# A macaron block on one core: 128 tokens left unturned at the end, one table load moved, queries and keys rounded for both heads at once

## The chip, the core and the metric

The kernel runs on one core of a Trainium2 chip. The metric is the device time of one execution in microseconds (us). TensorE does the matrix products (PE in the profile, PEld for its weight loads), VectorE (DVE) and ScalarE (ACT) the elementwise work, GpSimd (POOL) a little, and SyncE (SP) issues most of the transfers (DMAs) between HBM and the on-chip memory SBUF, and within SBUF. Products land in PSUM.

## What is computed

One transformer block over 512 tokens of width 1024, in float32: half a SwiGLU feed-forward, an attention mixer, half a second feed-forward, and a last norm.

```python
x = x + 0.5 * swiglu(rmsnorm(x, ffn1_norm), w_gate1, w_up1, w_down1)
x = x + token_mixer(rmsnorm(x, mix_norm), w_in, w_out, lambdas, subln_gain, rel_bias)
x = x + 0.5 * swiglu(rmsnorm(x, ffn2_norm), w_gate2, w_up2, w_down2)
return rmsnorm(x, final_norm)      # out: [1, 512, 1024]
```

The mixer has four differential heads (two softmaxes of 64-wide queries and keys each, the second subtracted with a learned factor) and eight dilated heads of width 64. All are causal, with a bias by distance. In the kernel they are eight pairs of 64-wide heads, `u` = 0 to 7: the first four pairs are the differential heads, the last four are the dilated ones.

## The kernel before

**Number format.** Every float32 value is kept as two parts: a high part rounded to the fast float32r format (`A.copy` into a float32r tile, a CAST in the profile) and a low part, value minus high (a subtraction on VectorE). A product of two values takes three TensorE passes (`mm3`, L152 to L154). Residual `x` lies transposed: eight tiles `x[m]` of 128 features by 512 tokens. Tokens 0 to 255 are the slice `left`, tokens 256 to 511 the slice `right`.

**Order.** TensorE's order is the order in which the code is written, everywhere. In the mixer VectorE's and ScalarE's is too; there the code runs through numbered chunks (`put(t, rank, ...)` hangs a step on chunk `t`, and steps with rank under 10 come ahead of the chunk's products, in order of rank). One unit of eight chunks makes the queries and keys of a pair (`q0` to `q7`), or half of the values (`v0` to `v3`), in the order v0 q0 q1 v1 q2 q3 q4 v2 q5 q6 v3 q7. A chunk is some 1.3 to 1.5 us of TensorE. The queues of SP and GpSimd are ordered by the framework's scheduler; each issues in that order, and a transfer that must wait holds what is behind it.

**Queries and keys of a pair.** `qk_chunks(u)` forms them. With `e` the pair's last chunk, `scaled` (L1055, L1057) writes `tq` and `tk`, 128 partitions by 512 tokens: partitions 0 to 63 (`lo`) belong to head 0 and 64 to 127 (`hi`) to head 1. The scores need six tiles. `q0` holds head 0's high part in `lo` and its low part in `hi`; `q1` the same for head 1 with the halves exchanged. `k0` and `k1` hold one head's high part in both halves, `l0` and `l1` its low part in both halves. So one pass over 128 partitions multiplies both parts of the query with the key's high part (L1227), and a second one with its low part (L1228). The tiles were filled in three ways:

- pairs 1 to 4 (`evac_q`, `evac_k`, `evac_rests`): each head by itself, 64 partitions at a time; four casts on ScalarE, four subtractions on VectorE, all written where they belong, and four SBUF-to-SBUF transfers (L1073) for the second halves of `k` and `l`;
- pairs 5 and 6 (`SPREAD`): keys rounded for both heads at once into `kh` and `kl` and sent by eight transfers (L1109); queries a head at a time in place;
- pairs 0 and 7 (`evac_now`): no transfers.

The first scores of a pair (`score`) stand at chunk `e` + 6, in `attention`. The softmax follows, with exponentials on ScalarE (L1232), weights turned by TensorE (`turn`, into `pt`), copied to `ptb` by ScalarE (L1256), and multiplied with the values (`values`, L1267).

**The last FFN and the end.** The second FFN ends with three plain products p5, p6, p7 (one output tile each) and four units `d` by a seven-product scheme. `squared` adds the squares for the last norm as each `x[m]` becomes final. Its root is a Sqrt on ScalarE, whose table differs from that of Silu, so a one-element Sqrt into `root` brought the table in ahead of time, after the square of tile 1. In `final_end` the 256 `left` tokens were scaled as they lie, features on partitions (`final_left`; the factors spread over partitions by a product with ones, `final_spread`), and stored transposed, so that the host turned them. The 256 `right` tokens were turned by 16 TensorE transposes (`final_turn`), scaled out of PSUM (`final_right`) and stored as rows.

Of the kernel before, what the change touches and what calls it, by code (L numbers as in the profile page):

```python
# [21 lines left out]
P = 128  # L22
# [60 lines left out]
def tile_macaron(ctx: ExitStack, tc, xs, xT, wf, wgu1, wst1, wd1, wdg1, wqk, wv, wo, wgu2, wst2, wd2,  # L83
# [153 lines left out]
    def ffn(wgu, wst, wd, wdg, n0, n1, norm, early, res, nm, hooks, ended, first=None,  # L237
# [426 lines left out]
        def schedule():  # L664
            seen = {}
            for t, (u, o) in enumerate(ops):
# [4 lines left out]
                else:  # L671
# [26 lines left out]
                    else:  # L698
                        at(starts[t] - 3 * STEP, 2.5, low, t)
                at(starts[t], 4, product, t)  # L700
            if bias is not None:
                at(starts[begin["p", 5]], 5, bias[0])
                at(starts[begin["p", 7]], 5, bias[1])
                at(starts[begin["p", 6]] + STEP, 5, bias[3])
                at(starts[begin["d", 1, 0] + 2], 5, bias[2])
# [327 lines left out]
    def qk_chunks(u):  # L1033
# [25 lines left out]

        def evac_q():  # L1060
            q0, q1, k0, k1, l0, l1 = tiles()
            tq, tk = scaled()
            A.copy(k0[lo, :], tk[lo, :])
            A.copy(k1[hi, :], tk[hi, :])
            A.copy(q0[lo, :], tq[lo, :])
            A.copy(q1[hi, :], tq[hi, :])

        def evac_k():
            q0, q1, k0, k1, l0, l1 = qk[u]
            tq, tk = st["tq"], st["tk"]  # L1070

            def other_half(t, a, b):
                nc.sync.dma_start(t[b, :].bitcast(F32), t[a, :].bitcast(F32))  # L1073

            other_half(k0, lo, hi)
            other_half(k1, hi, lo)
            for a, b, kx, lx in ((lo, hi, k0, l0), (hi, lo, k1, l1)):
                V.tensor_tensor(lx[a, :], tk[a, :], kx[a, :].bitcast(F32), op=ALU.subtract)
                other_half(lx, a, b)

        def evac_rests():
            q0, q1, k0, k1, l0, l1 = qk[u]
            tq = st["tq"]
            for a, b, qx in ((lo, hi, q0), (hi, lo, q1)):
                V.tensor_tensor(qx[b, :], tq[a, :], qx[a, :].bitcast(F32), op=ALU.subtract)

        def evac_now():
# [15 lines left out]
        elif u in DIRECT:  # L1103
            put(e, 11, evac_now)
        elif u in SPREAD:
            def send(t, *places):
                for o, a in zip(places, (lo, hi)):
                    for b in (lo, hi):
                        nc.sync.dma_start(o[b, :].bitcast(F32), t[a, :].bitcast(F32))  # L1109

            def cast_k():
                q0, q1, k0, k1, l0, l1 = tiles()
                t = st["kh"] = slot(0, f"kh{u}", F32R)
                A.copy(t[:], st["tk"][:])
                send(t, k0, k1)

            def low_k():
                q0, q1, k0, k1, l0, l1 = qk[u]
                t = slot(1, f"kl{u}", F32R)
                V.tensor_tensor(t[:], st["tk"][:], st["kh"][:].bitcast(F32), op=ALU.subtract)  # L1120
                send(t, l0, l1)

            def cast_q(n):
                a = (lo, hi)[n]
                A.copy(qk[u][n][a, :], st["tq"][a, :])

# [76 lines left out]
    def attention(u, s):  # L1203
# [205 lines left out]
        for i in range(NQ):  # L1409
# [320 lines left out]
    def final_dg():  # L1730
        n = NQ // 2
        dg = fin["dg"] = tp.tile([P, S], F32, tag="ptb", name="dgl")
        V.tensor_tensor(dg[:, :HS].rearrange("p (i q) -> p i q", i=n),
                        ident[:].rearrange("p (o q) -> p o q", o=1).to_broadcast([P, n, P]),
                        fin["y", 0][:].rearrange("p (i o) -> p i o", o=1).to_broadcast([P, n, P]),
                        op=ALU.mult)

    def final_spread():
        fin["pb"] = pp.tile([P, S], F32, tag="mm", name="bcl", bufs=4)[:, :HS]
        for c in (slice(0, P), slice(P, HS)):  # L1740
            T.matmul(fin["pb"][:, c], ones_m, fin["dg"][:, c], start=True, stop=True)


    def final_left(a):
        if a != 3:
            fin["left"] = wp.tile([P, 1024], F32, tag="raw", name=f"yl{a}")
        y = fin["left"][:, a // 3 * S:a // 3 * S + S].rearrange("p (m q) -> p m q", m=2)
        x2 = x_all[:, 2 * a * S:2 * (a + 1) * S].rearrange("p (m q) -> p m q", m=2)[:, :, left]
        f = fin["pb"].rearrange("p (o q) -> p o q", o=1).to_broadcast([P, 2, HS])
        V.tensor_tensor(y, x2, f, op=ALU.mult)  # L1750
        if a != 2:
            n = 1 + a // 3
            nc.sync.dma_start(out[0, 2 * (a + 1) - 2 * n:2 * (a + 1)].rearrange("m p q -> p m q"),
                              fin["left"][:, :n * S].rearrange("p (m q) -> p m q", q=HS))


    def final_turn(i, ms):
        for m in ms:
            h = m // 4
            if (i, h) not in fin:  # L1760
                tag = {(0, 0): "mm", (1, 0): "s", (0, 1): "s", (1, 1): "t"}[i, h]
                fin[i, h] = pp.tile([P, S], F32, tag=tag, name=f"xt{i}{h}", bufs=4 if tag == "mm" else 2)
            T.transpose(fin[i, h][:, m % 4 * P:(m % 4 + 1) * P],
                        x[m][:, HS + i * P:HS + (i + 1) * P], ident[:])
# [10 lines left out]

    def wd_tile(i):
        return tp.tile([P, 1280], F32, tag=f"pr{i}", name=f"yr{i}")

    def final_store(i, c, queue):
        o = out[1].rearrange("k p q -> (k p q)").rearrange("(t d) -> t d", d=D)  # L1780
        queue.dma_start(o[i * P:(i + 1) * P, c], fin["out", i][:, c])

    def final_end():
        q6, q7 = fin["sq"]
        every = slice(0, S)
        weigh(KD - 1, right, V)
        weigh(KD - 2, right)
        final_means(1, sq, end=False)
        final_spread()
        final_turn(0, range(2))  # L1790
        final_means(1, q6, first=False)
        final_left(0)
        final_roots(1)
# [6 lines left out]
        final_left(1)  # L1800
        final_right(0, 1, every, A)
        final_store(0, slice(0, D), nc.sync)
        final_left(2)
        final_left(3)
        final_right(1, 0, every, A)
        final_store(1, every, nc.sync)
        final_right(1, 1, right, V)
        final_right(1, 1, left, A)
        final_store(1, slice(S, D), nc.scalar)

# [112 lines left out]
```

## Time and profile before

| what | value |
|---|---|
| time, median of 3 runs | 890.2 us (889.88 to 890.86) |
| the profiled execution's own time | 890.6 us |
| its span in the profile | 887.7 us |
| HBM read, written | 137.28 MB, 2.14 MB |
| granted TensorE clock, mean | 0.997 of full speed |

Rows of a timeline give the start (us from the span's start), the duration, the engine, the line, the operation with output <- inputs, and in brackets how long the engine stood idle before it and for whom. Rows of waits give who waited <- for whom: us in total, times, longest. Rows of a group give minimum/median/maximum in ns, or in `--lines` form the busy us, mean ns, and idle time before. Rows of `windows` give a stretch, then the busy time of each engine, the granted clock, the share of the transfer engines' time and GB/s.

### The profile page before, as it was taken

To read this page: it belongs to the slowest core of one execution; us is meant where nothing else is said; L and a number is where in the kernel's file an instruction comes from. 1 tells how busy PE (TensorE), PEld (TensorE's weight loads), DVE (VectorE), ACT (ScalarE), POOL (GpSimd) and SP (SyncE) were. 2 spreads that over 40 slices of the span, in tenths; PEclk is the share of its full clock that TensorE was granted. 3 is DMA by queue.
4 is the path that set the end of the run, shared out by engine and by line. 5 is a ranking of instruction groups with operands and counts; after the bars stand their busy time and mean duration, and the time that the engine had idled before them with its cause. 6 is when DMAs were issued, how large, how long until landed. Compare 5 with 4: busy or idle time off the path is not lost.

```text
span 887.7 us, 17743 instructions
## 1 busy us (share of the span) xinstructions
PE 875.6 (99%) x6558; PEld 834.5 (94%) x6558; DVE 755.1 (85%) x1590; ACT 550.7 (62%) x1162; POOL 111.2 (13%) x140
## 2 busy tenths in 40 slices
PE   9999999999999999999999999999999999999996
PEld 8889999999999999998989889889999999999996
DVE  7799998787998995788997859999899678799786
ACT  7456674455765764666766858466667355666474
POOL 0011101012103100001010220011110111211100
PEclk9999999999999999999999999999999999999998
DMA  8456756688857842445365664656783857884842
GB/s 279 125 168 157 177 142 184 148 212 213 201 141 211 222 132 95 119 131 156 106 174 149 183 139 120 176 158 152 185 212 97 201 169 187 216 224 118 215 127 95
DMA packets 65685, 146.85 MB, mean 165 GB/s; under 512 B 7632, under 2 KB 8912, under 8 KB 65600
## 3 DMA queue, kind: packets, MB, share of 16 engines
q1 hardware_dynamic: 47840, 113.02, 39.2%
q0 software_dynamic: 17616, 32.45, 22.7%
q8 instruction: 51, 0.84, 0.4%
q14 instruction: 34, 0.28, 0.1%
q10 hardware_dynamic: 144, 0.26, 0.1%
HBM read 137.28 MB, written 2.14 MB: 157 GB/s over the span
## 4 chain that ended last, share of the span: by engine, by line
PE 82%; DVE 10%; ACT 4%; issue 2%; DMA 1%; SPq 0%; DVEq 0%; ACTq 0%
PE po L1267 2%; PE pdb L154 1%; DVE w L948 1%; PE pdb L153 1%; PE pdb L152 1%; DVE w L445 1%; PE pv L1012 1%; PE pv L1014 1%; PE pv L1013 1%; PE pygb L152 1%; PE pwgb L154 1%; PE pxgb L154 1%; PE pyub L154 1%; PE pyub L153 1%; PE pxub L154 1%
## 5 line engine op out<-in xcount | busy, mean ns | idle before, releaser
L1232 ACT ACTIVATE pr<-pr,small 128x128 f32<-128x128 f32 (+3 forms) x64 | 35.7, 559 | 31.4 <-DVE small L1229 31.1
L441 ACT CAST w<-s2b 128x512 fp32r<-128x512 f32 x52 | 32.4, 623 | 22.0 <-DVE s2b L423 19.9
L441 ACT CAST w<-s2a 128x512 fp32r<-128x512 f32 x48 | 29.8, 623 | 23.3 <-DVE s2a L423 19.7
L445 DVE TENSOR_TENSOR w<-s2b,w 128x512 fp32r<-128x512 f32 x52 | 35.6, 685 | 0.9 <-ACT w L441 0.6
L1012 PE MATMUL pv<-w,xh 128*128 128x256 f32 x128 | 35.7, 279 | 0.0
L1229 DVE CUSTOM_DVE_ANT_0 pr<-sc,strip 128x128 f32<-128x128 f32 (+3 forms) x64 | 29.5, 485 | 7.2 <-PE sc L1228 7.0
L1014 PE MATMUL pv<-w,xh 128*128 128x256 f32 x128 | 35.1, 274 | 0.0
L1013 PE MATMUL pv<-w,xl 128*128 128x256 f32 x128 | 35.1, 274 | 0.0
L445 DVE TENSOR_TENSOR w<-s2a,w 128x512 fp32r<-128x512 f32 x48 | 32.8, 684 | 0.8 <-ACT w L441 0.6
L152 PE MATMUL pq<-xh,w 128*128 128x512 f32 x64 | 25.6, 401 | 0.0
L948 DVE TENSOR_TENSOR w<-raw_qk,w 128x512 fp32r<-128x512 f32 x32 | 21.7, 686 | 4.5 <-ACT w L944 4.5
L1013 PEld LDWEIGHTS pv<-w,xl 128*128 128x128 f32 x128 | 24.5, 191 | 0.1
L1012 PEld LDWEIGHTS pv<-w,xh 128*128 128x128 f32 x128 | 24.5, 191 | 0.1
L1014 PEld LDWEIGHTS pv<-w,xh 128*128 128x128 f32 x128 | 24.5, 191 | 0.0
L152 PE MATMUL pk<-xh,w 128*128 128x512 f32 x64 | 24.3, 380 | 0.0
L154 PE MATMUL pq<-xh,w 128*128 128x512 f32 x64 | 24.3, 379 | 0.0
L153 PE MATMUL pk<-xl,w 128*128 128x512 f32 x64 | 24.3, 379 | 0.0
L154 PE MATMUL pk<-xh,w 128*128 128x512 f32 x64 | 24.3, 379 | 0.0
L153 PE MATMUL pq<-xl,w 128*128 128x512 f32 x64 | 24.3, 379 | 0.0
L1267 PEld LDWEIGHTS po<-v,ptb 128*128 128x128 f32 x160 | 21.5, 191 | 2.6 <-ACT ptb L1256 1.6
L944 ACT CAST w<-raw_qk 128x512 fp32r<-128x512 f32 x32 | 19.3, 615 | 6.2 <-PE pv L1013 2.8
L1267 PE MATMUL po<-v,ptb 128*128 128x128 f32 (+1 forms) x160 | 22.0, 272 | 1.0 <-ACT ptb L1256 1.0
(826 smaller groups left out, 4096.5 us busy)
## 6 DMA issues: line engine op xcount, KB each, us to landing
raw_qk<-wqk_dram SPq DMA_DIRECT2D x16, 512.0 KB, 3.8
raw0bg<-wst_dram SPq DMA_DIRECT2D x9, 512.0 KB, 5.0
raw0bu<-wst_dram SPq DMA_DIRECT2D x9, 512.0 KB, 5.7
raw_gua<-wgu_dram SPq DMA_DIRECT2D x8, 512.0 KB, 3.6
raw0ag<-wst_dram SPq DMA_DIRECT2D x8, 512.0 KB, 5.0
raw0au<-wst_dram SPq DMA_DIRECT2D x8, 512.0 KB, 5.2
raw0ad<-wdg_dram SPq DMA_DIRECT2D x8, 512.0 KB, 5.9
strip<-bias_rows SPq DMA_DIRECT2D x16, 256.0 KB, 4.0
```

The source lines that it names most:

```text
L152: T.matmul(po, wh, mh, start=first, stop=False, skip_group_check=on)
L153: T.matmul(po, wh, ml, start=False, stop=False, skip_group_check=on)
L154: T.matmul(po, wl, mh, start=False, stop=last, skip_group_check=on)
L441: A.copy(made[t][0], source(t))
L445: V.tensor_tensor(l, source(t), h.bitcast(F32), op=ALU.subtract)
L948: V.tensor_tensor(l[:, c:c + 512], raw[:, c:c + 512], h[:, c:c + 512].bitcast(F32), op=ALU.subtract)
L1012: T.matmul(po, xh[k][:, xs], mh_, start=k == 0, stop=False)
L1013: T.matmul(po, xl[k][:, xs], mh_, start=False, stop=False)
L1014: T.matmul(po, xh[k][:, xs], ml_, start=False, stop=k == KD - 1)
L1229: V.tensor_tensor_reduce(out=o, in0=a, in1=b, op0=ALU.add, op1=ALU.min, scale=1.0, scalar=3.0e38, accum_out=st["mx"][:, m, i:i + 1])
L1232: A.activation(pi, pi, AF.Exp, scale=-1.0, bias=st["mx"][:, m, i:i + 1], accum_out=st["ls"][:, m, i:i + 1])
L1267: T.matmul(st["po3"][:, i, d0:d0 + dn], st["ptb", m, i][:, k * P:(k + 1) * P], vk, start=k == 0, stop=k == i)
```

## The change

Four edits:

1. `root`'s one-element Sqrt, and the table load with it, moves from the square of tile 1 to the start of p6, after p6's products in the order of the code.
2. Pairs 1 to 6 all fill their tiles in one way. `cast_k` and `cast_q` round both heads at once, 128 partitions, into `kh` and `qh`; `low_k` and `low_q` subtract both at once into `kl` and `ql`. Everything is then placed by transfers: four for `kh`, four for `kl`, two for `qh`, two for `ql`, twelve for a pair. (Pairs 1 to 4 had four, pairs 5 and 6 eight.)
3. The first value products of pair 0 stand one chunk earlier.
4. At the end only tokens 0 to 127 stay unturned; tokens 128 to 511 are turned by 24 transposes. The output is one [512, 1024] array of rows, in which the first 128 rows hold the unturned block, re-ordered on the host.

```diff
@@ schedule, in ffn
+            if last is not None:
+                at(starts[begin["p", 6]], 5, lambda: A.activation(root[:], eps[:], AF.Sqrt))
@@ squared
             put(t + STEP, A.activation, sq[:], x[m], AF.Square)
-            if not mixer:
-                put(t + STEP, A.activation, root[:], eps[:], AF.Sqrt)
             put(t + 2 * STEP, weighted)
@@ qk_chunks
-        def evac_q():
...
-        def evac_k():
...
-        def evac_rests():
...
-        elif u in SPREAD:
+        else:
+            kt, lt, qt, rt = (20, 21, 22, 23) if u < 5 else (0, 1, 2, 3)
+
             def send(t, *places):
-                for o, a in zip(places, (lo, hi)):
-                    for b in (lo, hi):
-                        nc.sync.dma_start(o[b, :].bitcast(F32), t[a, :].bitcast(F32))
+                for a, o in zip((lo, hi), places):
+                    for p, b in o:
+                        nc.sync.dma_start(p[b, :].bitcast(F32), t[a, :].bitcast(F32))
 
             def cast_k():
                 q0, q1, k0, k1, l0, l1 = tiles()
-                t = st["kh"] = slot(0, f"kh{u}", F32R)
+                t = st["kh"] = slot(kt, f"kh{u}", F32R)
                 A.copy(t[:], st["tk"][:])
-                send(t, k0, k1)
+                send(t, ((k0, lo), (k0, hi)), ((k1, lo), (k1, hi)))
...
-            def cast_q(n):
-                a = (lo, hi)[n]
-                A.copy(qk[u][n][a, :], st["tq"][a, :])
-
-            def low_q(n):
-                a, b = ((lo, hi), (hi, lo))[n]
-                V.tensor_tensor(qk[u][n][b, :], st["tq"][a, :], qk[u][n][a, :].bitcast(F32),
-                                op=ALU.subtract)
+            def cast_q():
+                q0, q1 = qk[u][:2]
+                t = st["qh"] = slot(qt, f"qh{u}", F32R)
+                A.copy(t[:], st["tq"][:])
+                send(t, ((q0, lo),), ((q1, hi),))
+
+            def low_q():
+                q0, q1 = qk[u][:2]
+                t = slot(rt, f"ql{u}", F32R)
+                V.tensor_tensor(t[:], st["tq"][:], st["qh"][:].bitcast(F32), op=ALU.subtract)
+                send(t, ((q0, hi),), ((q1, lo),))
 
             put(e, 11, scaled)
             put(e + 1, 6.7, cast_k)
+            put(e + 2, 6.7, cast_q)
             put(e + 2, 7, low_k)
-            for n in range(2):
-                put(e + 2 + n, 6.7, cast_q, n)
-                put(e + 3 + n, 11, low_q, n)
-        else:
-            put(e, 11, evac_q)
-            put(e + 1, 11, evac_k)
-            put(e + 2, 7, evac_rests)
+            put(e + 3, 7, low_q)
@@ attention
-                put(tv + 2 * i + (3 if (u, i) in ((0, 0), (1, NQ - 1)) else 2), 1, values, 0, i)
+                put(tv + 2 * i + (3 if (u, i) == (1, NQ - 1) else 2), 1, values, 0, i)
@@ the end
+        y = wp.tile([P, 1024], F32, tag="raw", name=f"yl{a}")[:, :S]
+        x4 = x_all[:, 4 * a * S:4 * (a + 1) * S].rearrange("p (m q) -> p m q", m=4)[:, :, :P]
...
+        V.tensor_tensor(y.rearrange("p (m q) -> p m q", m=4), x4, f, op=ALU.mult)
+        nc.sync.dma_start(out[:P, a * S:(a + 1) * S], y)
@@ final_end
         weigh(KD - 1, right, V)
-        weigh(KD - 2, right)
+        final_turn(1, range(4))
+        final_spread()
         final_means(1, sq, end=False)
-        final_spread()
-        final_turn(0, range(2))
         final_means(1, q6, first=False)
         final_left(0)
+        final_rows(1, 0, A)
+        final_store(1, 0, nc.sync)
+        final_left(1)
         final_roots(1)
-        final_turn(0, (2, 3, 4, 5, 7))
...
+        weigh(KD - 2, right)
+        final_turn(1, range(4, 8))
+        final_turn(2, range(4))
+        final_turn(3, range(4))
+        final_turn(2, (4, 5, 7, 6))
+        final_turn(3, (4, 5, 7, 6))
         final_factors(1)
-        final_right(0, 0, every, A)
...
+        final_rows(1, 1, A)
+        final_store(1, 1, nc.sync)
+        final_rows(2, 0, V)
+        final_store(2, 0, nc.sync)
+        final_rows(3, 0, V)
+        final_rows(2, 1, A)
+        final_store(2, 1, nc.sync)
+        final_store(3, 0, nc.sync)
+        final_rows(3, 1, V, right)
+        final_rows(3, 1, A, left)
+        final_store(3, 1, nc.scalar)
```

`_OUT_SHAPE` and the host's last lines follow the new layout.

**SP's queue at pair 1, before.** The rows are the transfers that SP issues between two weight loads of the mixer (`raw_qk`); `k` and `l` are the key tiles, a number names a buffer, and `strip` is a bias strip of a later pair.

```order
L139 DMA raw_qk_4672<-wqk_dram 128x1024
L1073 DMA k_4457<-k_4457 64x512
L1073 DMA k_4458<-k_4458 64x512
L1073 DMA l_4459<-l_4459 64x512
L1073 DMA l_4460<-l_4460 64x512
L878 DMA strip_4882<-bias_rows 128x512
L878 DMA strip_4884<-bias_rows 128x512
L139 DMA raw_qk_4680<-wqk_dram 128x1024
```

**The same place after the change.** `q_4469` and `q_4470` are the query tiles of the two heads.

```order
L139 DMA raw_qk_4680<-wqk_dram 128x1024
L1083 DMA k_4471<-kh_4475 64x512 x2
L1083 DMA k_4472<-kh_4475 64x512 x2
L1083 DMA q_4469<-qh_4504 64x512
L1083 DMA q_4470<-qh_4504 64x512
L1083 DMA l_4473<-kl_4508 64x512 x2
L1083 DMA l_4474<-kl_4508 64x512 x2
L1083 DMA q_4469<-ql_4546 64x512
L1083 DMA q_4470<-ql_4546 64x512
L139 DMA raw_qk_4688<-wqk_dram 128x1024
L880 DMA strip_4894<-bias_rows 128x512
L880 DMA strip_4896<-bias_rows 128x512
```

Four transfers became twelve, and the low halves of the queries are the last two. Two strips and a load of weights stand behind them.

**ScalarE at pair 1, before.** These are its casts of keys and queries, among the exponentials of pair 0 (`pr`) and the copy of turned weights (`ptb`).

```order
L1232 ACTIVATE pr_4379,small_4380<-pr_4379,small_4380 128x256
L1063 CAST k_4457<-tk_4462 64x512
L1064 CAST k_4458<-tk_4462 64x512
L1065 CAST q_4455<-tq_4461 64x512
L1066 CAST q_4456<-tq_4461 64x512
L1232 ACTIVATE pr_4378,small_4380<-pr_4378,small_4380 128x384
L1232 ACTIVATE pr_4379,small_4380<-pr_4379,small_4380 128x384
L944 CAST w<-raw_qk_4412 128x512
L1256 COPY ptb_4503<-pt_4501 128x128
```

**The same place after the change.**

```order
L1204 ACTIVATE pr_4379,small_4380<-pr_4379,small_4380 128x256
L1204 ACTIVATE pr_4378,small_4380<-pr_4378,small_4380 128x384
L1204 ACTIVATE pr_4379,small_4380<-pr_4379,small_4380 128x384
L1088 CAST kh_4475<-tk_4456 128x512
L944 CAST w<-raw_qk_4412 128x512
L1228 COPY ptb_4499<-pt_4497 128x128
L1100 CAST qh_4504<-tq_4455 128x512
```

Two casts of 128 partitions took the place of four of 64; the first stands behind two exponentials that it stood ahead of, and the second behind the copy. In the same stretch TensorE's order differs only in the value product of pair 0 that stands a chunk earlier; its scores of pair 1 stand where they stood.

More of the change, by code (lines that the diff above doesn't have):

```diff
@@ L1058, in scaled @@
             return tq, tk
-        def evac_q():
[L1061 to L1066, printed above, removed]
-        def evac_k():
[L1069 to L1079, printed above, removed]
-        def evac_rests():
[L1082 to L1085, printed above, removed]
         def evac_now():
@@ L1111, in cast_k @@
             def cast_k():
                 q0, q1, k0, k1, l0, l1 = tiles()
-                t = st["kh"] = slot(0, f"kh{u}", F32R)
+                t = st["kh"] = slot(kt, f"kh{u}", F32R)
                 A.copy(t[:], st["tk"][:])
-                send(t, k0, k1)
+                send(t, ((k0, lo), (k0, hi)), ((k1, lo), (k1, hi)))
             def low_k():
                 q0, q1, k0, k1, l0, l1 = qk[u]
-                t = slot(1, f"kl{u}", F32R)
+                t = slot(lt, f"kl{u}", F32R)
@@ L1120, in low_k @@
                 V.tensor_tensor(t[:], st["tk"][:], st["kh"][:].bitcast(F32), op=ALU.subtract)
-                send(t, l0, l1)
-            def cast_q(n):
-                a = (lo, hi)[n]
-                A.copy(qk[u][n][a, :], st["tq"][a, :])
-            def low_q(n):
-                a, b = ((lo, hi), (hi, lo))[n]
-                V.tensor_tensor(qk[u][n][b, :], st["tq"][a, :], qk[u][n][a, :].bitcast(F32),
-                                op=ALU.subtract)
+                send(t, ((l0, lo), (l0, hi)), ((l1, lo), (l1, hi)))
@@ L1730, in final_dg @@
     def final_dg():
-        n = NQ // 2
         dg = fin["dg"] = tp.tile([P, S], F32, tag="ptb", name="dgl")
[L1733 to L1736, printed above, removed]
+        V.tensor_scalar_mul(dg[:, :P], ident[:], fin["y", 0][:, 0:1])
     def final_spread():
-        fin["pb"] = pp.tile([P, S], F32, tag="mm", name="bcl", bufs=4)[:, :HS]
-        for c in (slice(0, P), slice(P, HS)):
-            T.matmul(fin["pb"][:, c], ones_m, fin["dg"][:, c], start=True, stop=True)
+        fin["pb"] = pp.tile([P, S], F32, tag="mm", name="bcl", bufs=4)[:, :P]
+        T.matmul(fin["pb"], ones_m, fin["dg"][:, :P], start=True, stop=True)
     def final_left(a):
[L1745 to L1754, printed above, removed]
+        y = wp.tile([P, 1024], F32, tag="raw", name=f"yl{a}")[:, :S]
+        x4 = x_all[:, 4 * a * S:4 * (a + 1) * S].rearrange("p (m q) -> p m q", m=4)[:, :, :P]
+        f = fin["pb"].rearrange("p (o q) -> p o q", o=1).to_broadcast([P, 4, P])
+        V.tensor_tensor(y.rearrange("p (m q) -> p m q", m=4), x4, f, op=ALU.mult)
+        nc.sync.dma_start(out[:P, a * S:(a + 1) * S], y)
     def final_turn(i, ms):
@@ L1760, in final_turn, with final_rows @@
             if (i, h) not in fin:
-                tag = {(0, 0): "mm", (1, 0): "s", (0, 1): "s", (1, 1): "t"}[i, h]
+                tag = {(1, 0): "mm", (1, 1): "s", (2, 0): "s", (2, 1): "t", (3, 0): "t", (3, 1): "mm"}[i, h]
                 fin[i, h] = pp.tile([P, S], F32, tag=tag, name=f"xt{i}{h}", bufs=4 if tag == "mm" else 2)
             T.transpose(fin[i, h][:, m % 4 * P:(m % 4 + 1) * P],
-                        x[m][:, HS + i * P:HS + (i + 1) * P], ident[:])
-    def final_right(i, h, c, engine):
-        ps, f = fin[i, h], fin["y", 1][:, i:i + 1]
+                        x[m][:, i * P:(i + 1) * P], ident[:])
+    def final_rows(i, h, engine, c=slice(0, S)):
+        ps, f = fin[i, h], fin["y", i // 2][:, i % 2:i % 2 + 1]
         if ("out", i) not in fin:
-            fin["out", i] = wd_tile(i)
+            fin["out", i] = tp.tile([P, 1280], F32, tag=f"pr{i % 2}", name=f"yr{i}")
         y = fin["out", i][:, h * S:(h + 1) * S]
@@ L1774, in final_right, with final_store @@
             V.tensor_scalar_mul(y[:, c], ps[:, c], f)
[L1776 to L1781, printed above, removed]
+    def final_store(i, h, queue):
+        c = slice(h * S, (h + 1) * S)
+        queue.dma_start(out[i * P:(i + 1) * P, c], fin["out", i][:, c])
     def final_end():
         q6, q7 = fin["sq"]
-        every = slice(0, S)
         weigh(KD - 1, right, V)
-        weigh(KD - 2, right)
+        final_turn(1, range(4))
+        final_spread()
         final_means(1, sq, end=False)
-        final_spread()
-        final_turn(0, range(2))
         final_means(1, q6, first=False)
         final_left(0)
+        final_rows(1, 0, A)
+        final_store(1, 0, nc.sync)
+        final_left(1)
         final_roots(1)
-        final_turn(0, (2, 3, 4, 5, 7))
-        final_turn(1, range(4))
-        final_turn(0, (6,))
-        final_turn(1, (4, 5, 7, 6))
-        final_factors(1)
-        final_right(0, 0, every, A)
[L1800 to L1809, printed above, removed]
+        weigh(KD - 2, right)
[4 more added lines that the diff above has]
+        final_turn(3, (4, 5, 7, 6))
+        final_factors(1)
+        final_rows(1, 1, A)
[9 more added lines that the diff above has]
+        final_store(3, 1, nc.scalar)
     n3 = {}
@@ L1818 @@
         "lams", "relb", "onehot", "addc"]
-_OUT_SHAPE = [2, KD, P, S // 2]
+_OUT_SHAPE = [S, D]
 def _bucket(n):
@@ L1921 @@
     y = r.results[0]["out_0_dram"]
-    return np.concatenate([np.roll(y[0], 1, axis=0).reshape(D, S // 2).T, y[1].reshape(S // 2, D)])[None]
+    first = np.roll(y[:P].reshape(P, KD, P), 1, axis=1).transpose(2, 1, 0).reshape(P, D)
+    return np.concatenate([first, y[P:]])[None]
```

1 line of the change is left out of this document (removed).

## The prediction

> **What bounds the kernel.** I read the busy line of the page, then TensorE's waits, then the chain that ended last, and after them the rows around each wait.
>
> ```profile
> PE 875.6 (99%) x6558; PEld 834.5 (94%) x6558; DVE 755.1 (85%) x1590; ACT 550.7 (62%) x1162; POOL 111.2 (13%) x140
> ...
> PE po L1267 <- ACT ptb L1256: 1.0, 2, 0.5
> PE pt L1350 <- DVE tx L1358: 0.5, 1, 0.5
> PE pt L1250 <- DVE tx L1358: 0.3, 1, 0.3
> PE pydb L152 <- ACT pydb L470: 0.3, 1, 0.3
> ...
> 847.30 1.27 ACT L470
> ```
>
> TensorE is busy for 99% of 887.7 us, and its order of work is written out by hand. So work saved on VectorE or ScalarE is worth only what it removes from TensorE's own waits, and those are small: 1.0 + 0.5 + 0.3 us in the mixer and 0.3 us in the last FFN. The last row is the unnamed 1.27 us at the head of a ScalarE chain near the end: the table load before `root`. Anything that makes TensorE wait anew costs its full length, since no idle time later takes it back.
>
> **The terms that gain.** These are the rows where TensorE stands still in the mixer and at the table load.
>
> ```profile
> 370.19 0.71 PE L1267 MATMUL po<-v,ptb 128*128 128x128 f32 x4 [0.47 <-ACT ptb L1256]
> 413.06 0.49 PE L1267 MATMUL po<-v,ptb 128*128 128x128 f32 x2 [0.51 <-ACT ptb L1256]
> 481.63 0.52 PE L1350 MATMUL pt<-ident,pr 128*128 128x128 f32 x3 [0.53 <-DVE tx L1358]
> 852.97 0.38 PE L152 MATMUL pydb<-h3b,w 128*128 128x256 f32 x1 [0.32 <-ACT pydb L470]
> 829.07 0.62 ACT L608 CAST h3b<-g0b 128x512 fp32r<-128x512 f32 x1 [2.32 <-DVE g0b L479]
> ...
> L1063 ACT CAST k<-tk x4: 617/619/621, 362.4 to 422.4; 64x512 fp32r<-64x512 f32 x4
> L1114 ACT CAST kh<-tk x2: 601/610/620, 457.8 to 472.2; 128x512 fp32r<-128x512 f32 x2
> L1078 DVE TENSOR_TENSOR l<-tk,k x8: 680/688/691, 363.2 to 423.8; 64x512 fp32r<-64x512 f32 x8
> ```
>
> A cast over 64 partitions costs 0.62 us and one over 128 costs 0.61; the subtraction is 0.69 either way. Pairs 1 to 4 go from four casts and four subtractions to two and two, pairs 5 and 6 save one of each: 10 x 0.62 = 6.2 us of ScalarE and 10 x 0.69 = 6.9 us of VectorE. Nearly all of it lies beside TensorE. What counts is that the copy of `ptb` which holds up 370.19 and 413.06, and the `tx` which holds up 481.63, each move up by 0.6 to 1.3 us, so these three waits go. Only the third is a clean gain, **-0.5 us**; the first two sit just ahead of new waits and are counted there. The (0,0) values go one chunk earlier; their `ptb` copy moves up with the casts that no longer stand before it, so I cost that at nothing. The table load leaves 847.30 and stands beside a row that had 2.32 us of idle time before it: **-0.4 us** (0.32 and the refill behind it), and 1.3 us of late casts there if that idle time is gone.
>
> **The term that costs: twelve transfers on one queue.** All of them go through SP.
>
> ```profile
> L1109 SPq DMA_DIRECT2D k<-kh x8: 467/573/602, 458.4 to 474.6; - x8
> L1109 SPq DMA_DIRECT2D l<-kl x8: 467/562/589, 461.2 to 477.2; - x8
> ...
> DMA to landing us min/median/max: 2.3/2.4/4.7
> ...
> L139 SPq DMA_DIRECT2D raw_qk<-wqk_dram x16: 327/330/1126, 322.3 to 463.9; - x16
> ...
> 458.42 2.40 SPq L1109 DMA_DIRECT2D k<-kh  x4
> 472.82 2.40 SPq L1109 DMA_DIRECT2D k<-kh  x4
> ```
>
> These sends exist already for pairs 5 and 6. Four in a row take 2.40 us, so SP issues one each 0.60 us, and each lands 2.4 us after its issue. Before, a pair had four or eight; now every one of pairs 1 to 6 has twelve: 40 more, 24 us of SP time. The score of head 0 reads the whole query tile, high half and low half, so it cannot start before the eleventh send has landed: 10 x 0.60 + 2.4 = 8.4 us after `kh` is cast, and head 1's 9.0 us. In the old form queries never left the engines, and the keys needed only four sends. TensorE's order is the same, so its scores stand where they stood. These rows give the end of `tk` and the first score of each pair (for 1 to 3 that of head 1 too).
>
> ```profile
> 361.64 0.68 DVE L1057 TENSOR_TENSOR tk<-pk,rbc_n 128x512 f32<-128x512 f32 x1
> 371.31 0.28 PE L1227 MATMUL sc<-k,q 128*128 128x256 f32 x1
> 392.28 0.68 DVE L1057 TENSOR_TENSOR tk<-pk,rbc_n 128x512 f32<-128x512 f32 x1
> 400.12 0.28 PE L1227 MATMUL sc<-k,q 128*128 128x256 f32 x1
> 400.36 0.28 PE L1227 MATMUL sc<-k,q 128*128 128x256 f32 x1
> 406.67 0.68 DVE L1057 TENSOR_TENSOR tk<-pk,rbc_n 128x512 f32<-128x512 f32 x1
> 416.02 0.39 PE L1227 MATMUL sc<-k,q 128*128 128x256 f32 x1
> 421.67 0.69 DVE L1057 TENSOR_TENSOR tk<-pk,rbc_n 128x512 f32<-128x512 f32 x1
> 432.23 0.28 PE L1227 MATMUL sc<-k,q 128*128 128x256 f32 x1
> 464.70 0.28 PE L1227 MATMUL sc<-k,q 128*128 128x256 f32 x1
> 481.90 0.37 PE L1227 MATMUL sc<-k,q 128*128 128x256 f32 x1
> ...
> L1232 ACT ACTIVATE pr<-pr,small 128x384 f32<-128x384 f32 x12 | 7.3, 611 | 5.2 <-DVE small L1229 5.1
> L1307 ACT ACTIVATE mh<-ot,few 128x512 fp32r<-128x512 f32 x4 | 2.8, 691 | 0.0
> L1256 ACT COPY ptb<-pt x11: 252/369/586, 366.6 to 418.9; 128x128 f32<-128x128 f32 x3, 128x256 f32<-128x256 f32 x3, 128x384 f32<-128x384 f32 x3, 128x512 f32<-128x512 f32 x2
> ```
>
> - Pair 1: `tk` ends at 362.3; `kh` now stands behind two exponentials of 0.61, which start half a microsecond later, so it ends near 364.7. Head 1's last send lands at 364.7 + 9.0 = 373.7, against a score at 371.31: **+2.4**.
> - Pair 2: `tk` ends at 393.0, and `kh` is behind the copy of `ptb` (0.59) and `mh` (0.69), which wait for TensorE until about 392.5: 394.4. Head 1 lands at 403.4, against 400.36: **+3.0**.
> - Pair 3: `tk` ends at 407.35 and `kh` at 408.0, so 417.0 against 416.02, +1.0. But VectorE's backlog ahead of this `tk` shrinks by about the microsecond, and then it is nothing. I take **+0.5**.
> - Pair 4: `kh` ends at about 424.0 behind a copy of `ptb`; the cast of the queries is behind two exponentials, at 426.9, and SP stands for it. Six sends follow before head 0's last: 426.9 + 6 x 0.60 + 2.4 = 432.9 against 432.23, **+0.7**. Head 1's score is chunks later.
> - Pair 5: the first send stands at 458.42, so 466.8 against 464.70: **+2.1**.
> - Pair 6: 472.82 + 8.4 = 481.2 against 481.90: **0**.
>
> Together +8.7 us (2.4 + 3.0 + 0.5 + 0.7 + 2.1). While a score waits, everything behind it on TensorE waits; VectorE and ScalarE run ahead and then starve. The weight loads and bias strips that queue behind the sends on SP come up to 7 us later, but they are read a whole pair later, so I cost them at nothing.
>
> For bounds: at the fastest issue (0.47) and the 2.3 landing the waits shrink to +0.9, +1.5, -0.5, 0 and +0.7, +2.6 in all (10 x 0.47 + 2.3 = 7.0 after `kh` for head 0, 7.5 for head 1); at the slowest landing (4.7) five heads would add 11.5. The medians stand for sends in a row, which these are, so I take 0.60 and 2.4.
>
> **The tail.**
>
> ```profile
> 878.60 1.73 PE L1763 MATMUL xt<-ident,x 128*128 128x128 f32 x14
> ...
> 878.88 2.03 SPq L1753 DMA_DIRECT2D out_dram<-yl  x2
> ...
> 882.61 0.38 ACTq L1781 DMA_DIRECT2D out_dram<-yr  x1
> ...
> 882.00:884.00 2.00, 0.00 (x0) 0.00 (x0) 0.07 (x1) 0.47 (x1) 0.00 (x0) 0.80 1.02 388
> 886.00:888.00 2.00, 0.00 (x0) 0.00 (x0) 0.00 (x0) 0.00 (x0) 0.00 (x0) 0.50 0.07 26
> ...
> 883.00:883.50 0.50, 0.00 (x0) 0.00 (x0) 0.00 (x0) 0.00 (x0) 0.00 (x0) 0.70 0.91 367
> ```
>
> The end is bound by the 2.1 MB of output: at 388 GB/s 256 KB take 0.67 us, and most of it is issued after 881. Now four blocks (two `yl`, and rows 1 with the factors that are known already) go out from 878.9 on, where the first store stands now, and the last issue falls from 882.61 to about 882.0. The transposes after the sum go from 14 to 20, 0.7 us more, beside the factors. Eight blocks of 0.67 from 879.6 end near 885.0; before, data flowed until about 886.2 (the row from 886 on has 26 GB/s for two microseconds, 52 KB): **-1.2 us**, between 0 and -2.
>
> **Sum:** +8.7 - 0.5 - 0.4 - 1.2 = **+6.6 us**. On the profiled execution's own 890.6 (span 887.7 and 2.9 around it) that is 897.2; that execution is 0.4 above the median of the runs, 890.2, so the forecast is **896.8 us**.
>
> **Rivals.**
> 1. *The sends are in time* (ends faster). If SP issued them as fast as its weight loads, 0.33 us, head 0 would have its queries 3.3 + 2.4 = 5.7 us after `kh`: 370.4, 400.1 and 464.1 for pairs 1, 2 and 5, no later than the scores. All gains would stay: 0.6 at 370, 1.2 at 413 and the two scores behind it (416.02 stands 0.6 later than its chunk needs), then 0.5 + 0.4 + 1.2 as above: 3.9, so 886.3 us. It decides at an issue of about 0.35. The rows of the sends, 0.56 to 0.60, speak against it. 8%. [...]
> 2. *Every send is as short as the shortest seen* (0.47, 2.3): +2.6 - 2.1 = +0.5, 890.7 us. 15%.
> 3. *The clock falls in the new waits.* The granted clock went to half at 883.2 (mean 0.70 in the last row), 2.9 us after the last transpose at 880.3. The waits of pairs 1 and 2 are 2.6 to 2.7 us long, just short of it. If they count, TensorE runs at half for about as long and loses some 1.5 us each time, at two or three places: 900 to 901 us. 12%. [...]
> 4. *Landing nearer its maximum*, because twelve sends crowd each other: above 901. 5%.
>
> **How the numbers follow.** My case, 893 to 900, has 60%. The range from 889.8 to 902.0 takes in most of rivals 2 and 3. About 0.2% is what a measurement of this kernel can tell from no change. Faster by more (under 888.4): rival 1 and a little of 2, 0.09. Within it: most of 2, 0.11. Slower (above 892.0): 0.80.
>
> **What would show it.** In the changed profile TensorE's first score of pairs 1, 2 and 5 waits 2 to 3 us for a DMA, with twelve sends of 0.6 us on SP just before. Waits on `ptb` at 370 and 413 are gone, `pydb` no longer waits near 853, and the output is stored about a microsecond sooner after the last product. I am wrong if the sends are issued in 0.3 to 0.4 us each, or if scores start at the same distance from `tk` as before.

## The result, and the profile after

| | before | changed |
|---|---|---|
| time, median | 890.04 us (889.77 to 890.86) | **916.63 us** (914.78 to 918.03) |
| the profiled execution's own time, its span | 890.6, 887.7 us | 917.04, 915.0 us |
| granted TensorE clock, mean | 0.997 | 0.985 |

The ratio is 1.0295, with an interval of 1.0283 to 1.0307: slower, as forecast, but by 26.6 us and not by 6.6, and far outside the range. First the busy line, the slice row of the granted clock and TensorE's longest waits of the changed kernel (a wait's columns are who waited <- for whom: us, times, longest).

```profile
PE 887.5 (97%) x6564; PEld 845.2 (92%) x6564; DVE 748.7 (82%) x1580; ACT 544.5 (60%) x1152; POOL 111.1 (12%) x140
...
PEclk9999999999999999997998999999999999999999
```

```profile
PE sc L1199 <- DMA q<-ql: 20.0, 6, 4.3
...
PE pt L1222 <- DVE tx L1330: 0.3, 1, 0.3
```

The waits on `ptb` and on the table load are gone, and VectorE and ScalarE have less to do (755.1 to 748.7 and 550.7 to 544.5 us), as the change says. In their place stands one new wait, the one that was forecast, with 20.0 us and not 8.7. TensorE's busy time grows by 12 us although it has only six products more: it ran more slowly, at a mean granted clock of 0.985 against 0.997. The first score of each pair, from the timeline (start, duration, and in brackets the wait):

```profile
374.82 0.47 PE L1199 MATMUL sc<-k,q 128*128 128x256 f32 x1 [4.32 <-DMA q<-ql]
409.88 0.55 PE L1199 MATMUL sc<-k,q 128*128 128x256 f32 x1 [4.10 <-DMA q<-ql]
430.69 0.55 PE L1199 MATMUL sc<-k,q 128*128 128x256 f32 x1 [3.86 <-DMA q<-ql]
451.75 0.35 PE L1199 MATMUL sc<-k,q 128*128 128x256 f32 x1 [1.65 <-DMA q<-ql]
488.20 0.58 PE L1199 MATMUL sc<-k,q 128*128 128x256 f32 x1 [4.08 <-DMA q<-ql]
508.05 0.55 PE L1199 MATMUL sc<-k,q 128*128 128x256 f32 x1 [2.03 <-DMA q<-ql]
```

All six pairs wait. Now the twelve sends on SP's queue for pair 1 and for pair 6 (rows of the timeline; "x4" is four in a row).

```profile
364.67 2.44 SPq L1083 DMA_DIRECT2D k<-kh  x4
367.15 1.25 SPq L1083 DMA_DIRECT2D q<-qh  x2
368.50 3.67 SPq L1083 DMA_DIRECT2D l<-kl  x4
372.27 1.19 SPq L1083 DMA_DIRECT2D q<-ql  x2
...
499.32 2.39 SPq L1083 DMA_DIRECT2D k<-kh  x4
501.81 1.19 SPq L1083 DMA_DIRECT2D q<-qh  x2
503.09 2.48 SPq L1083 DMA_DIRECT2D l<-kl  x4
505.67 1.19 SPq L1083 DMA_DIRECT2D q<-ql  x2
```

Pair 6 is the pace that the prediction took: a send each 0.6 us, and the score starts 8.76 us after `kh` (which ended at 499.29; 8.4 were predicted). In pair 1 the four of `l` take 1.2 us longer, and the score starts 10.17 us after `kh`. Its `kh` ended at 364.65; those of pairs 2 to 5 ended at 399.75, 419.28, 441.64 and 477.65, so there it is 10.13, 11.41, 10.11 and 10.55 us.

Last, the clock around the waits. These are windows at which the granted clock changes (stretch, length, TensorE busy, granted clock, share of the transfer engines' time, GB/s).

```profile
374.75:375.00 0.25, 0.18 (x1) 0.82 1.37 172
378.25:378.50 0.25, 0.25 (x4) 0.86 0.28 107
409.00:409.50 0.50, 0.00 (x0) 0.54 0.84 225
415.50:416.00 0.50, 0.50 (x3) 0.63 0.65 90
429.50:430.00 0.50, 0.00 (x0) 0.52 1.09 336
436.00:436.50 0.50, 0.50 (x3) 0.65 0.78 229
450.00:453.50 3.50, 1.85 (x16) 1.00 0.92 257
487.50:488.00 0.50, 0.00 (x0) 0.55 1.04 221
494.00:494.50 0.50, 0.50 (x3) 0.62 0.00 0
508.00:508.50 0.50, 0.45 (x2) 0.53 1.15 242
511.00:511.50 0.50, 0.50 (x4) 0.56 0.00 0
```

A window that is part full and part half clock gives the moment: the clock reads 1.00 from 408.5 to 409.0 and 0.50 from 409.5 to 415.5, so 0.54 from 409.0 to 409.5 means that it fell at 409.04. So it fell at 374.91, 409.04, 429.52, 487.55 and 508.03, and rose at 378.32, 415.87, 436.35, 494.38 and 511.44. It fell behind five of the six waits and stayed at half for 3.4 to 6.8 us; only pair 4, with 1.65 us, kept it. At 0.50 products of 128x512 start 0.43 us apart (433.15, 433.58, 434.00), at 1.00 0.22 us (436.57, 436.79, 437.00). So from each resumption to the rise half the time is lost at most, an estimate from these stretches: 1.7, 3.0, 2.8, 3.1 and 1.7, together 12 us.

### The profile page after: what moved, and what is told of

The parts are those of the page before. It is cut to its first block, busy times and chain, and to the rows that moved or that the text cites. A ratio compares the mean times of both kernels' runs of the same rounds, so it can differ in the third digit from the quotient of the medians.

```text
span 915.0 us, 17819 instructions
## 1 busy us (share of the span) xinstructions
PE 887.5 (97%) x6564; PEld 845.2 (92%) x6564; DVE 748.7 (82%) x1580; ACT 544.5 (60%) x1152; POOL 111.1 (12%) x140
## 4 chain that ended last, share of the span: by engine, by line
PE 82%; DVE 8%; ACT 3%; DMA 2%; issue 2%; SPq 1%; DVEq 0%; ACTq 0%
DMA q<-ql 2%; PE po L1239 2%; SPq L1083 1%; PE pq L152 1%; PE pdb L152 1%; PE pq L154 1%; PE pdb L153 1%; PE pdb L154 1%; PE pq L153 1%; DVE w L445 1%; PE pk L153 1%; PE pk L152 1%; PE pk L154 1%; PE sc L1199 1%; PE pv L1011 1%
## 5 line engine op out<-in xcount | busy, mean ns | idle before, releaser
L1199 PE MATMUL sc<-k,q 128*128 128x256 f32 (+2 forms) x64 | 23.7, 375 | 20.0 <-DMA q<-ql 20.0
L1011 PE MATMUL pv<-w,xh 128*128 128x256 f32 x128 | 36.8, 287 | 0.0
L1013 PE MATMUL pv<-w,xh 128*128 128x256 f32 x128 | 36.2, 283 | 0.0
L1199 PEld LDWEIGHTS sc<-k,q 128*128 128x128 f32 x64 | 13.4, 209 | 22.9 <-issue 13.2
L152 PE MATMUL pq<-xh,w 128*128 128x512 f32 x64 | 27.2, 424 | 0.0
L1011 PEld LDWEIGHTS pv<-w,xh 128*128 128x128 f32 x128 | 25.6, 200 | 0.1
L1013 PEld LDWEIGHTS pv<-w,xh 128*128 128x128 f32 x128 | 25.6, 200 | 0.0
L154 PE MATMUL pq<-xh,w 128*128 128x512 f32 x64 | 25.5, 399 | 0.0
L152 PE MATMUL pk<-xh,w 128*128 128x512 f32 x64 | 25.5, 399 | 0.0
L154 PE MATMUL pk<-xh,w 128*128 128x512 f32 x64 | 25.4, 397 | 0.0
```

Source lines behind the costliest of these rows:

```text
L152: T.matmul(po, wh, mh, start=first, stop=False, skip_group_check=on)
L154: T.matmul(po, wl, mh, start=False, stop=last, skip_group_check=on)
L1011: T.matmul(po, xh[k][:, xs], mh_, start=k == 0, stop=False)
L1013: T.matmul(po, xh[k][:, xs], ml_, start=False, stop=k == KD - 1)
L1199: T.matmul(ps[:, :n], qs[:, qi], mk, start=True, stop=False)
```

## The experiments

Each kernel was timed against the kernel before, on the same chip. The ratios are to those runs. A gain or a loss in us is the difference of the two medians; the ratio's distance from 1, times 890, agrees with it within 0.3 us (0.6 in r9).

**r1, the old queries and keys.** The changed kernel with edit 2 undone:

```diff
+    SPREAD = (5, 6)
...
+        def evac_q():
...
+        def evac_k():
...
+        def evac_rests():
...
-        else:
-            kt, lt, qt, rt = (20, 21, 22, 23) if u < 5 else (0, 1, 2, 3)
-
+        elif u in SPREAD:
...
-            put(e + 2, 6.7, cast_q)
             put(e + 2, 7, low_k)
-            put(e + 3, 7, low_q)
+            for n in range(2):
+                put(e + 2 + n, 6.7, cast_q, n)
+                put(e + 3 + n, 11, low_q, n)
+        else:
+            put(e, 11, evac_q)
+            put(e + 1, 11, evac_k)
+            put(e + 2, 7, evac_rests)
```

> The changed kernel with the queries and keys of pairs 1 to 6 made as before (edit 2 undone; the turned tail, the moved table load and the earlier first value stay). Theory: edit 2 is all of the loss, and the other edits bring about 1.7 us at the end (before, 12.72 us from the last wait on st_n to the end; after, 11.03) and 0.3 us at the table load: 888.0 us, 887.4 to 888.8. Rival A: those two bring nothing that lasts, 889.7 to 890.4. Rival B: a part of the 27 us belongs to them: above 892.

Measured: 889.1 us (887.48 to 890.31), ratio 0.9986, 0.9977 to 0.9995. All of the loss is edit 2. The other three together gain 1.0 us (1.2 by the ratio), between what the theory and its rival A expected.

**r2, the waits filled.** Products that nothing reads, ahead of the first score:

```diff
+            if i == m == 0:
+                for _ in range({1: 16, 2: 16, 3: 15, 5: 16, 6: 7}.get(u, 0)):
+                    T.matmul(ps[:], xh[0][:, :P], full(xh[0][:]), start=True, stop=True)
             T.matmul(ps[:, :n], qs[:, qi], mk, start=True, stop=False)
```

> The changed kernel with 16, 16, 15, 16 and 7 products that nothing needs ahead of the first score of pairs 1, 2, 3, 5 and 6, 0.215 us each at full clock, so that TensorE works through most of each wait (4.32, 4.10, 3.86, 4.08, 2.03 us). Theory: the waits themselves (20 us) stay, but the clock no longer falls behind them; half clock held for 3.4, 5.8, 5.4, 6.0 and 3.4 us after them and cost half of that, 12 us at most, so 904.5 to 908 us and a mean granted clock of 0.995 or more. Rival: the clock falls for another reason (the transfers, the load), and the products change nothing: 914 to 919 us.

Measured: 907.1 us (906.61 to 907.93), ratio 1.0194, 1.0180 to 1.0208; mean clock 0.998 to 0.999, and 1.00 from 300 to 560 us, where all the waits for sends lie. Its wait for the sends, and the first score of pair 4:

```profile
PE sc L1202 <- DMA q<-ql: 5.3, 6, 1.6
```

```profile
444.82 0.36 PE L1202 MATMUL sc<-k,q 128*128 128x256 f32 x1 [0.98 <-DVE yt_a L191]
```

The 70 products fill 70 x 0.215 = 15.0 us, and 5.3 us of waiting are left, with another 1.0 at pair 4. (The profile puts that one down to `yt_a`, but the score starts 2.5 us after the first send of `ql` is issued at 442.30, as that of pair 1 does after the change, from 372.27 to 374.82.) That makes 21.3 us, against 20.0 in the changed kernel. TensorE is held up for no less, yet 9.5 us are back (916.63 - 907.1). That is the price of the falls of the clock, separated from the waits.

**r3, two queues.** The queries' sends from ScalarE's queue:

```diff
-            def send(t, *places):
+            def send(t, *places, queue=nc.sync):
...
-                send(t, ((q0, lo),), ((q1, hi),))
+                send(t, ((q0, lo),), ((q1, hi),), queue=nc.scalar)
...
-                send(t, ((q0, hi),), ((q1, lo),))
+                send(t, ((q0, hi),), ((q1, lo),), queue=nc.scalar)
```

> The changed kernel with the four sends of the queries issued by ScalarE's queue, the eight of the keys by SP. Theory 1, SP's issue is what paces the sends (0.60 us each): eight are left on it, so each first score waits some 2.4 us less, and most falls of the clock go too: 896 to 903 us. Theory 2, the transfer engines pace them (in pair 1's sends they are 0.8 to 0.9 busy at 200 to 215 GB/s, which is 128 KB each 0.6 us): the same bytes take the same time whoever issues them, 912 to 919 us.

Measured: 911.19 us (908.54 to 913.38), ratio 1.0235, 1.0215 to 1.0255: between the two, and neither range is met. The windows say why. First a stretch of pair 1's sends in r3, before the next load of weights is issued at 370.66, then one of pair 6's in the changed kernel:

```profile
368.50:369.50 1.00, 1.00 0.93 254
369.50:370.50 1.00, 1.00 1.02 246
```

```profile
501.00:507.00 6.00, 1.00 0.87 204
```

From one queue, sends of 128 KB keep the transfer engines busy for 0.87 of the time, at 204 GB/s; from two, for 0.93 to 1.02 of it at 246 to 254. The second queue has little room left, and what it issues sooner lands later: the median send of r3 lands after 3.4 us, that of the changed kernel after 2.5.

**r4, only the keys sent.** Queries rounded a head at a time in place, as pairs 5 and 6 had it:

```diff
...
-            put(e + 2, 6.7, cast_q)
...
-            put(e + 3, 7, low_q)
+            for n in range(2):
+                put(e + 2 + n, 6.7, cast_q, n)
+                put(e + 3 + n, 11, low_q, n)
```

> The changed kernel with the queries of pairs 1 to 6 rounded a head at a time in place, as pairs 5 and 6 had it; only the eight sends of the keys are left. Both theories take 2.4 us and more off each wait: 4.3, 4.1, 3.9, 1.7, 4.1 and 2.0 become about 1.2, 1.0, 0.8, 0, 1.0 and 0, and none is long enough for the clock: 890 to 894 us. Should 8 sends cost as much as 12, it would stay above 910.

Measured: 892.3 us (891.02 to 893.36), ratio 1.0024, 1.0013 to 1.0035. Its wait for the sends:

```profile
PE sc L1198 <- DMA l<-kl: 4.1, 6, 1.1
```

Of the 26.6 us of loss 2.2 are left, or 3.2 against r1, which has the same end and table load. The waits on `l` are 4.1 us in all, the longest 1.1, and the clock (0.997 to 0.999) does not fall behind them. The four sends of the queries, the last ones of each pair, were most of the loss.

**r5, halved sends.** Twice as many, the same bytes:

```diff
-                        nc.sync.dma_start(p[b, :].bitcast(F32), t[a, :].bitcast(F32))
+                        for n in (0, 32):
+                            nc.sync.dma_start(p[b.start + n:b.start + n + 32, :].bitcast(F32),
+                                              t[a.start + n:a.start + n + 32, :].bitcast(F32))
```

> The changed kernel with each of the twelve sends of a pair cut in two of 32 partitions: 24 sends, the same bytes, the same 2 KB rows. Theory 2 (the transfer engines pace the sends, 128 KB in 0.6 us): each half takes 0.3 us, the twelve still take 8 to 9 us, and the time stays near that of the change, 912 to 922 us. Theory 1 (SP needs its 0.5 to 0.6 us for a send of any size): 24 sends take 12 to 14 us, each of six waits grows by 4 to 6 us and the clock falls behind all of them: 940 to 955 us.

Measured: 958.74 us (956.55 to 960.2), ratio 1.0769, 1.0752 to 1.0785: theory 1, and a little more. Its sends (ns, minimum/median/maximum), its wait for them, and a window of its transfers:

```profile
L1084 SPq DMA_DIRECT2D k<-kh x48: 512/586/2196, 365.1 to 537.3; - x48
L1084 SPq DMA_DIRECT2D l<-kl x48: 534/588/590, 374.4 to 545.2; - x48
```

```profile
PE sc L1201 <- DMA q<-ql: 57.3, 8, 11.3
```

```profile
371.00:378.00 7.00, 0.72 0.41 103
```

A send of 64 KB takes SP 0.588 us, one of 128 KB 0.595 (the median of `l` in the changed kernel). The transfer engines are busy for only 0.41 of the time now. So SP's time for a send was the same for 64 and for 128 KB, and the number of sends on one queue was what counted. With 128 KB the two limits lie close together: 0.59 us of issue, and an estimate of 0.53 us of transfer (131,072 bytes at r3's 246 GB/s). That is why a second queue gained only 5.4 us (r3) and fewer sends gained nearly all (r4).

**r6, no other transfers beside the sends.** The sums `mx` of pairs 0 to 3 on VectorE:

```diff
-            if u == 6:
+            if u < 4 or u == 6:
                 V.tensor_tensor(w[:], mh[u][:].bitcast(F32), ml[u][:].bitcast(F32), op=ALU.add)
```

> The changed kernel in which the sum mx of pairs 0 to 3 is one subtraction-sized addition on VectorE (0.69 us) instead of two transfers of 256 KB by GpSimd's queue. Theory: these transfers meet the sends of pairs 2, 3 and 5 (landings of 2.7 to 3.9 us there, 2.3 in pair 6, where nothing else runs); without them the waits of these three shrink by about 1 us each, from 4.1, 3.9 and 4.1, and each of the clock's falls behind them may become shorter: 908 to 914 us. Rival: the landings are late for another reason, and it stays at 914.5 to 918 us.

Measured: 907.63 us (905.61 to 910.47), ratio 1.0199, 1.0181 to 1.0217, a little better than expected. The sends of `l` in pairs 2 and 5, first in the changed kernel, then in r6:

```profile
403.53 3.35 SPq L1083 DMA_DIRECT2D l<-kl  x4
...
481.46 3.47 SPq L1083 DMA_DIRECT2D l<-kl  x4
```

```profile
403.52 2.58 SPq L1083 DMA_DIRECT2D l<-kl  x4
...
477.76 2.47 SPq L1083 DMA_DIRECT2D l<-kl  x4
```

The stretched sends of these two pairs are gone, and the waits of pairs 2, 3 and 5 fall to 2.8, 2.4 and 2.2 us. So beside GpSimd's transfers the four sends of `l` held SP longer in these two pairs, by 0.77 and 1.00 us. The waits of pairs 1 and 4 did not shrink: 4.6 and 2.4 us, against 4.3 and 1.7. Pairs 1, 3 and 4 keep a stretched send in r6. There the transfers of the changed kernel show something else (from the part on DMA, 364 to 376, and windows of pair 1):

```profile
q8 instruction: 1, 0.02, 0.8%
```

```profile
368.50:369.00 0.50, 1.00 0.89 197
369.00:370.50 1.50, 1.00 0.41 93
370.50:371.00 0.50, 1.00 0.20 57
371.00:372.00 1.00, 1.00 0.90 207
```

One packet of instructions took 0.8% of 16 engines in 12 us, 1.5 us of one engine, and right behind it the transfers fall to 0.41 and then to 0.20 of the time, 93 and 57 GB/s. Pairs 3 and 4 have a packet of the same size beside their sends, pair 2 a smaller one, pairs 5 and 6 none. That is a coincidence in time over six pairs and two kernels; that the packet is the cause is not shown.

r6 also shows a wait that brought no fall of the clock. The first score of pair 3:

```profile
427.03 0.36 PE L1199 MATMUL sc<-k,q 128*128 128x256 f32 x1 [2.43 <-DMA q<-ql]
```

In the mixer the clock of r6 first falls at 374.86, and the next falls (409.00, 446.54, 484.09, 501.16) follow by 34.14, 71.68, 109.23 and 126.30 us, which are 10, 21, 32 and 37 times 3.413 us; those of the changed kernel lie on such a grid too. By that count (374.86 + 15 x 3.413) one step of the grid ends at 426.06, in the middle of this wait: 1.46 us of it lie before, 0.97 behind, and the clock stays at 1.00. Pair 5 waited less, 2.19 us, but 1.95 of them lie in one step, and the clock fell at its end, at 484.09.

**r7, the scores later.** `5 + 3 * (w in ("q1", "q2", "q3"))` for the 5 chunks between a pair and its attention.

> The changed kernel with the attention of pairs 1, 2 and 3 three chunks (some 4.2 us) later in the written order, so that other products stand where TensorE waited. Theory: the waits of 4.3, 4.1 and 3.9 us become 0 to 0.3 each, and the falls of the clock behind them (3.4, 5.8 and 5.4 us at half) go with them, worth 12 + 7 us: 896 to 901 us. Rival: what follows the scores is late in their place (the exponentials, the weights' copies, the values), and half of it or more comes back: 905 to 912 us.

Measured: 900.62 us (899.12 to 902.8), ratio 1.0120, 1.0106 to 1.0134, at the upper end of the theory. **r9** does the same to r4, one chunk later.

> The kernel of r4 (keys sent, queries in place) with the attention of pairs 1, 2 and 3 one chunk (about 1.4 us) later. Theory: the 4.1 us for which its scores still waited on l (0.5 to 1.2 us each) go, and rounding the keys of both heads at once is then free: 887.6 to 889.2 us, as fast as with the old queries and keys (r1, 889.1). Rival: as in r7, what follows the scores is late in their place, and a part of the 4.1 us comes back: 889.5 to 892 us.

Measured: 892.64 us (892.02 to 895.88), ratio 1.0034, 1.0020 to 1.0047, no better than r4: the rival, and 0.6 us above its range. TensorE's waits in r7, then in r9:

```profile
PE sc L1199 <- DMA q<-ql: 6.0, 3, 2.2
PE pk L152 <- DVE mx L1351: 1.9, 1, 1.9
PE po L1341 <- DVE tq L1054: 1.7, 1, 1.7
PE pk L152 <- DVE tq L1054: 1.7, 1, 1.7
```

```profile
PE po L1339 <- DVE ob L1262: 1.8, 1, 1.8
...
PE pk L152 <- DVE tq L1054: 0.9, 1, 0.9
PE sc L1198 <- DMA l<-kl: 0.9, 2, 0.6
PE pt L1320 <- ACT ptb L1226: 0.8, 1, 0.8
PE pk L152 <- DVE ob L1262: 0.7, 1, 0.7
```

In r7 the waits of pairs 1 to 3 are gone; the 6.0 us are those of pairs 4 to 6 (1.7, 2.2 and 2.0), and its clock is 1.00 from 300 to 560 us. But later scores make what follows them late: in r9 the sends' 4.1 us became 0.9, and 4.2 us (1.8 + 0.9 + 0.8 + 0.7) came back elsewhere.

**r8, r10 and r11, the gains by themselves.** The kernel before with edit 4 alone, with edit 1 alone, and with both. Edit 1 is

```diff
+            if last is not None:
+                at(starts[begin["p", 6]], 5, lambda: A.activation(root[:], eps[:], AF.Sqrt))
...
-            if not mixer:
-                put(t + STEP, A.activation, root[:], eps[:], AF.Sqrt)
```

> The kernel before with edit 4 alone (only 128 tokens unturned). Theory: the end is 1.0 to 1.7 us sooner, as the predicted -1.2 and the traces (12.7 us from the last wait on st_n to the end before, 11.0 after) have it: 888.4 to 889.2 us. Rival: that gain is the clock's luck at the end of one execution, and it stays within 0.3 us of before: 889.8 to 890.4 us; the 1.0 us of r1 is then the table load's.

> The kernel before with edit 1 alone (the table load moved to p6). The prediction put it at -0.4 us: 889.4 to 889.9. Rival, from r1 and r8 (889.1 with edits 1, 3 and 4, 889.23 with 4 alone): nothing that can be measured, 889.9 to 890.3.

> The kernel before with edits 1 and 4 (table load and tail), without 2 and 3. Theory: r8 and r10 add up, 0.9 + 0.9 us: 888.0 to 888.8 us, and edit 3 cost r1 some half microsecond. Rival: they do not add up, and it equals r1, 888.9 to 889.3.

| | us | before | ratio |
|---|---|---|---|
| r8, tail | 889.23 (887.95 to 892.63) | 890.09 | 0.9991 (0.9982 to 1.0000) |
| r10, table load | 889.36 (888.95 to 890.25) | 890.22 | 0.9992 (0.9984 to 1.0001) |
| r11, both | **888.29** (887.8 to 889.45) | 889.93 | 0.9983 (0.9974 to 0.9991) |

They add up, 0.9 + 0.9 against 1.6 us, as far as such small terms can be told: the intervals of r8 and r10 reach to 1.0000 and 1.0001, so that neither gain by itself is clear of nothing. r11 is faster than both kernels. Against r1 (0.9986) it cannot be told what edit 3 costs or gains.

## Why the prediction was right in sign and wrong in size

1. **The term that failed** is "+8.7 us", and in it the step "the medians stand for sends in a row, which these are, so I take 0.60 and 2.4". The pace was right (r5: 0.59 a send, of 64 or of 128 KB) and undisturbed it gives 8.76 us for 8.4 (pair 6). But five pairs of six took 10.1 to 11.4: one send in twelve holds SP 0.9 to 1.2 us longer, and landings beside it take up to 4.8. That is 1.8, 1.7, 3.0, 1.2 and 2.2 us more for pairs 1 to 5 (pair 4 against 8.9, since its term began with 2.9 us until the queries are cast). These 9.9 us, with pair 6's 2.0, are 11.9, where the waits outgrew the forecast by 11.3; the places of the scores differ by some tenths. Part of it is GpSimd's transfers (r6). The profile before had no twelve sends in a row, only four; the median of four undisturbed ones was taken for twelve, with nothing for what they meet on the way. Rival 4, with 5%, had the late landings, but not the held-up issue.
2. **Pair 6 at 0** was a wrong row. The row at 481.90 is the score of its head 1. That of head 0 stands behind the three turns before those, as the score that waits at 508.05 does after the change:

```profile
479.02 0.49 PE L1350 MATMUL pt<-ident,pr 128*128 128x128 f32 x3
479.27 0.37 PE L1227 MATMUL sc<-k,q 128*128 128x256 f32 x1
```

   With the prediction's own 481.2 the term would have been +1.9; it measured 2.03.
3. **The falling clock** was a rival with 12%, "some 1.5 us each time, at two or three places". The sum put it at nothing. The falls came, the condition was wrong. It took 2.9 us of standing still, from one row, as what a fall needs; the clock fell after 2.0 us (pair 6) as well, at five places, and r2 prices it at 9.5 us. The rival also spoke of waits of 2.6 to 2.7 us, "just short of it", where the prediction's own sum has 2.4 and 3.0. Beside pair 6's 2.0 us even the forecast waits of pairs 1, 2 and 5 (2.4, 3.0 and 2.1 us) could have been long enough, had each lain within one step of the grid that r6 shows; that is an estimate from these falls.
4. **The rivals with faster sends.** Rival 1's pace, the 0.33 us of the weight loads, did not come: a send of 128 KB took 0.595 us, and one of half the bytes 0.588 (r5). Rival 2's +2.6 us counts pair 3's -0.5 as a gain; a score that could start sooner than its place gives nothing back, so that its sum is +3.1.
5. **The gains** came: waits on `ptb` at 370 and 413, on `tx` at 481 and on `pydb` at 853 are gone. (r1 still has 1.4 us of those on `ptb` and `tx`, so they went with edit 2.) The tail was put at -1.2 and measured -0.9 by itself (in the traces, 12.7 us from the last wait for a sum `st_n` to the end became 11.0); the table load at -0.4 and measured -0.9, with an interval that holds both, and nothing as well.
6. **Edit 3 and the freed 6 to 7 us of ScalarE and VectorE** were costed at nothing; r1 and r11 show no difference for edit 3, and r4 and r9, which keep a part of the freed time, are no faster than r1.

The sum of it: 20.0 us of waits and 9.5 of clock, less about 2 of gains, is the 27.3 us by which the span grew. Against the forecast of +6.6 that is 20.7 more: 11.3 of waits and 9.5 of clock.

## What to carry to other kernels

Count the sends that one queue must issue before the last operand is there, and not the engine time that they save: here engines that nobody waited for gave nothing back (r4 and r9, with a part of their time freed, took 892.3 and 892.64 us, r1 889.1), a send of 64 KB cost 0.588 us of issue and one of 128 KB 0.595, and what held the sends up on the way added 0.9 to 1.2 us in five pairs of six. Price a new wait on TensorE at its length, and ask for the clock behind it: here waits of 2.0 to 4.3 us brought five falls that cost 9.5 us, some 2 us each, but 2.4 us in r6 and 2.2 in r7 brought none. And before a score, a product or a copy is taken as the first of its group, follow it in the order of the program, or the slack is read from the wrong row.

## What the runs showed of the hardware that was not expected

- The five falls and five rises of the clock in the mixer lie on one grid of 3.41 us: 378.32 - 374.91 = 3.41, 415.87 - 409.04 = 6.83, 409.04 - 374.91 = 34.13, ten times 3.413. A step of that grid with 2.0 us of standing still out of 3.41 ended in a fall (pair 6; 1.95 us in r6), one with 1.65 us did not (pair 4), a wait of 2.43 us split over two steps brought none either (r6), and steps at half clock with 0.65 to 1.2 us of standing still (pairs 2, 3 and 5) did not end in a rise. What sets the grid is not shown.
- SP took as long to issue a send within SBUF of 32 partitions as of 64: medians of 0.588 us (r5) and 0.595 (the changed kernel). The core's transfer engines were busy for 0.87 of the time with 128 KB sends from one queue, at 204 GB/s, and for 0.93 to 1.02 of it with two queues, at 246 to 254 (r3).
